# Hymba-style layer on one core: bias rows replicated inside DRAM, set-up moved behind the first projection, down operands in low slots

## The chip, the cores and the metric

One Trainium2 chip, one of its cores. The time is device microseconds (us) of the whole kernel on that core. A matrix product runs on TensorE (PE), elementwise work on VectorE (DVE), ScalarE (ACT) and GpSimd (POOL). In this kernel every transfer is issued by SyncE (SP), on one hardware queue that spreads over the core's 16 DMA engines; the issue order on SP is the order in which each DMA engine gets its packets.

## What is computed

The reference is one decoder layer on 2048 tokens of 1024 features: an input projection, sliding-window attention beside RWKV-7 time mixing, an output projection, and a gated feed-forward part with a causal convolution of width 3. Cut to what matters here:

```python
h = rms_norm(x, norm_mix_pre)
proj = h @ w_in                                   # 1024 x 2560
q, k, v, p = split(proj, (512, 640, 768))         # attention part, then the RWKV part p
attn = sliding_window_sink_attention(q, k, v, rel_bias, sinks)
p = p + (shift(p) - p) * rwkv_shift_mix           # token shift, 14 groups of 128 columns
rw = rwkv7_time_mix(p, w0, w_decay_up, a0, w_iclr_up, w_gate_up, k_k, k_a, r_k, ln_x_g, ln_x_b)
x = x + rms_norm(concat(attn, rw) @ w_out, norm_mix_post)
f = conv_gated_ffn(rms_norm(x, norm_ffn_pre), w_ffn_up, conv_w, conv_b, w_ffn_down)
x = x + rms_norm(f, norm_ffn_post)

# inside the attention: a bias that depends on head and distance alone
bias = rel_bias[t5_bucket(rel)]                   # -1e30 outside the window of 128
```

## The kernel before

The kernel runs in stages. `phase_a` (L403 on) goes over four segments of 512 tokens; each takes 20 projections of 128 columns of `w_in` (eight of them as two halves of 64 columns in the attention part) and builds the inputs of the recurrence. `phase_b` (L900 on) does attention, the recurrence in chunks and the output projection; `phase_d` (L100 on) does the feed-forward product up (L244) and down (L392). The tile scheduler of the language orders the instructions of each engine after the code is written, so the row of an engine is not always the order of the source.

Every float32 product is made of three products of rounded parts: `split` casts a tile to its high part on ACT (L40) and subtracts on DVE to get the low part (L41). One projection `proj` (L544) loads a raw weight tile `wr` of 512 KB (L548, two buffers), splits it into `wh` and `wl`, and runs 24 matmuls into `pj` (L30). The hidden vectors of the segment are split into `hh` and `hl`.

The parts that are touched:

- `bias_lines` (L54 to L65), called at L802 before the first segment, makes one line of 384 bias values for each of 8 heads in `ln` (8 partitions), and L65 writes it 128 times over to DRAM, as `d_line` (8 x 128 x 384, 1.5 MB), with a copy whose source is broadcast from the 8 rows. `phase_b` reads `d_line` at L968, with a pitch of 383, so that each of 128 partitions gets its shifted line.
- The parameter vectors (`rows` L485, transposed at L488 into `vec`, with `half` and `omix` behind) and the low-rank weights `wraw` / `wup` / `wlo` / `wgh` / `wgl` (L500 to L515) are set up in `phase_a` ahead of the first projection.
- `shifted` (L556) evicts a projection on ACT: `ps<-pj` (L560), `t<-pj,omix` (L562). `load_x` (L455) squares, normalizes and transposes a tile of tokens: on ACT the squares `junk<-xt` (L467), on PE the transposes `hx` (L473). The step string loads the next segment's tokens (L464) late in a segment, in the steps x; in segment 0 the scheduler hoists the first of these loads, and the squares behind them, to the kernel's start.
- `pairs` (L648) writes `aa` and `bk` (one buffer each) and stores them with `d_ar` (L667) and `d_bk` (L672). `attn` (L765) makes one projection of the attention part; with i = 0 it transposes on PE (`sm`, L577) and stores `d_va` (L772).
- `dprep` (L159) splits the operands of the down product into slots of a list of big buffers, `OPL` (L134) alternating between two sets; `APL` (L346) names the slots that hold finished sums.

The order of segment 0's steps is this string (L807; z lowrank, K key, D decay, P pairs, V value, a attn, x load of the next tokens):

```python
A_ORDER = "z K D K D P a K D P K D P P x i V x i i i V x i i i V x i i i V i i a a a a a"
```

Of the kernel before, what the change touches and what calls it, by code (L numbers as in the profile page):

```python
# [14 lines left out]
P = 128  # L15
# [6 lines left out]
H = 8  # L22
# [16 lines left out]
def split(nc, hi, lo, raw):  # L39
    nc.scalar.copy(out=hi, in_=raw)  # L40
    nc.vector.tensor_tensor(out=lo, in0=raw, in1=hi, op=ALU.subtract)  # L41
# [9 lines left out]
    return r  # L51


def bias_lines(nc, pool, psum, rel_bias, onehot, neg, line_d):  # L54

    rb = pool("rb")[:32, :H]
    nc.sync.dma_start(out=rb, in_=rel_bias)
    oh = pool("oh")[:32, :384]
    nc.sync.dma_start(out=oh, in_=onehot)
    ln = pool("ln")[:H, :384]  # L60
    nc.sync.dma_start(out=ln, in_=bcast_rows(neg, H))
    pl = psum("pl")[:H, :384]
    nc.tensor.matmul(out=pl, lhsT=rb, rhs=oh, start=True, stop=True)
    nc.vector.tensor_tensor(out=ln, in0=pl, in1=ln, op=ALU.add)
    nc.sync.dma_start(out=line_d, in_=ln[:, None, :].to_broadcast([H, P, 384]))  # L65


def hsum(nc, pool, tag, h2t, hq, k):
# [26 lines left out]
def phase_d(ctx, tc, x1, h2t, w_up, cw, halo, w_down, g_post, mhalf, out, hq, act, td):  # L95
# [8 lines left out]
    with ExitStack() as es:  # L104
# [26 lines left out]
        x1v = x1.rearrange("(t p) d -> t p d", p=P)  # L131
        phases = [(p, k) for p in ORD for k in range(KC)]
        raw, dops = {}, {}
        OPL = ((0, 1, 2), (10, 11, 12))  # L134

        HPL = ((0, 1), (2, 3), (4, 5), (10, 11), (6, 7), (8, 9), (12, 13))

# [201 lines left out]
        with ExitStack() as ds_:  # L339
# [3 lines left out]
            nc.sync.dma_start(out=gpost, in_=bcast_rows(g_post))  # L343
            ssq = fp.tile([P, 2, SEQ // P], F32, name="ssq")
            xts, acc = {}, {}
            APL = {"C22": (3, 4), "C12": (5, 6), "C11": (7, 8)}  # L346

            def xload(t):
                xts[t] = fp.tile([P, D], F32, name="xt", bufs=3)
# [70 lines left out]
def phase_a(ctx, tc, x, g_pre, w_in, vecs, w_decay, w_iclr, w_gate, tri, ident, mhalf, gc, o, bias):  # L420
# [5 lines left out]
    with ExitStack() as es:  # L426
# [50 lines left out]
        for _ in load_x(0):  # L477
            pass


        rows = cp.tile([42, P], F32, name="rows")
        r0 = 0
        for v in vecs:
            n = v.shape[0] // P
            nc.sync.dma_start(out=rows[r0:r0 + n, :], in_=v.rearrange("(j p) -> j p", p=P))  # L485
            r0 += n
        pt = ps_s.tile([P, 512], F32, name="sm")
        nc.tensor.transpose(out=pt[:, :42], in_=rows, identity=ident[:42, :42])  # L488
        vec = cp.tile([P, 42], F32, name="vec")
        nc.vector.tensor_copy(out=vec, in_=pt[:, :42])  # L490
        hw0, ha0, k_k, k_a, r_k, ln_g, ln_b = (vec[:, 4 * i:4 * i + 4] for i in range(7))
        mix = vec[:, 28:42]
        half = cp.tile([P, 12], F32, name="half")
        nc.vector.tensor_scalar(out=half[:, 0:8], in0=vec[:, 0:8], scalar1=0.5, scalar2=None, op0=ALU.mult)
        nc.vector.tensor_scalar(out=half[:, 8:12], in0=k_a, scalar1=0.5, scalar2=None, op0=ALU.mult)
        hw0, ha0, hka = half[:, 0:4], half[:, 4:8], half[:, 8:12]
        omix = cp.tile([P, 14], F32, name="omix")
        nc.vector.tensor_scalar(out=omix, in0=mix, scalar1=-1.0, scalar2=1.0, op0=ALU.mult, op1=ALU.add)

        wl2, wup = [], []  # L500
        for h, w in ((0, w_decay), (1, w_iclr)):
            raw = ep.tile([P, 512], F32, tag="e", name="wraw", bufs=NE)
            nc.sync.dma_start(out=raw[0:64], in_=w)
            nc.sync.dma_start(out=raw[64:128], in_=w)
            hi = cp.tile([P, 512], F32R, name=f"wup{h}")
            nc.scalar.copy(out=hi, in_=raw)
            lo = cp.tile([P, 512], F32R, name=f"wlo{h}")
            nc.vector.tensor_tensor(out=lo, in0=raw, in1=hi, op=ALU.subtract)
            wl2.append(lo)
            wup.append(hi)  # L510
        raw = ep.tile([P, 512], F32, tag="e", name="wraw", bufs=NE)
        nc.sync.dma_start(out=raw, in_=w_gate)
        wgh = cp.tile([P, 512], F32R, name="wgh")
        wgl = cp.tile([P, 512], F32R, name="wgl")
        split(nc, wgh, wgl, raw)  # L515
        ind = cp.tile([P, 2], F32, name="ind")
        bones = cp.tile([P, P], F32, name="bones")
        nc.vector.memset(ind, 0.0)
# [16 lines left out]
        def segment(sb, nxt):  # L535
# [19 lines left out]

            def shifted(i, tag="sh", bufs=5):  # L556
                u = proj([768 + i * P])
                s = ep.tile([P, SB + 1], F32, name="ps", tag="ps", bufs=2)
                nc.scalar.copy(out=s[:, 0:1], in_=halo[:, i:i + 1])
                nc.scalar.copy(out=s[:, 1:], in_=u)  # L560
                t1 = E("t1", tag, bufs)
                nc.scalar.activation(out=t1, in_=u, func=AF.Copy, scale=omix[:, i:i + 1])  # L562
                nc.scalar.copy(out=halo[:, i:i + 1], in_=s[:, SB:])
                nc.vector.scalar_tensor_tensor(out=t1, in0=s[:, :SB], scalar=mix[:, i:i + 1], in1=t1, op0=ALU.mult, op1=ALU.add)
                return t1
# [19 lines left out]

            def lowrank():
                z = shifted(12)
                nc.scalar.activation(out=z[0:64], in_=z[0:64], func=AF.Tanh)
                zw = ep.tile([P, SB], F32R, name="zw")
                za = ep.tile([P, SB], F32R, name="za")  # L590
                nc.scalar.copy(out=zw[0:64], in_=z[0:64])
                nc.vector.tensor_tensor(out=zw[64:128], in0=z[0:64], in1=zw[0:64], op=ALU.subtract)
                nc.scalar.copy(out=za[64:128], in_=z[64:128])
                nc.vector.tensor_tensor(out=za[0:64], in0=z[64:128], in1=za[64:128], op=ALU.subtract)
                z = shifted(13)
                nc.scalar.activation(out=z, in_=z, func=AF.Tanh, scale=0.5)
                nc.vector.tensor_scalar(out=z, in0=z, scalar1=0.5, scalar2=0.5, op0=ALU.mult, op1=ALU.add)
                zgh = ep.tile([P, SB], F32R, name="zgh")
                zgl = ep.tile([P, SB], F32R, name="zgl")
                split(nc, zgh, zgl, z)  # L600
                lr.extend((zw, za, zgh, zgl))

            def decay(hp):
                zw, za = lr[:2]
                fs = slice(hp * P, (hp + 1) * P)
# [12 lines left out]
                ig = E("ig", "e", 6)  # L618
                nc.scalar.activation(out=ig, in_=cum, func=AF.Exp, scale=CDEC)
                nc.gpsimd.tensor_copy(out=gc[:, hp, cs], in_=ga[:, :, C])  # L620

                u = lora((wup[1][:, fs], za), (wl2[1][:, fs], za))
                ta = E("ta", "e", 6)
                nc.scalar.activation(out=ta, in_=u, func=AF.Tanh, scale=0.5, bias=ha0[:, c1])
                held[hp] = ga, ig, ta

            def key(hp):

                c1 = slice(hp, hp + 1)
# [55 lines left out]

            def value(hp):
                zgh, zgl = lr[2:]
                fs = slice(hp * P, (hp + 1) * P)
                c1 = slice(hp, hp + 1)

# [72 lines left out]
                    yield  # L763

            def attn(i):  # L765
                ts = slice(t0, t0 + SB)
                u = proj([[640], [512]][i] if i < 2 else [(i - 2) * 64, 256 + (i - 2) * 64])
                t = E("qkv", "qo", 2)
# [370 lines left out]
def hybrid_layer(ctx, tc, a, c, out):  # L1139
# [6 lines left out]
    nc.vector.memset(mhalf, -0.5)  # L1146
    gc = cp.tile([P, 4, SEQ // C], F32, name="gc")
    s = {k: dp.tile(list(v), F32, name="d_" + k) for k, v in A_OUT.items()}
    line = dp.tile([H, P, 384], F32, name="d_line")
    x1 = dp.tile([SEQ, D], F32, name="d_x1")  # L1150
    h2t = [dp.tile([8, P, SEQ // 2], F32, name=f"d_h2t{j}") for j in range(2)]
# [4 lines left out]
    x = a["x"][0]  # L1156
    vecs = [a[n].rearrange("l h n -> (l h n)") if n == "r_k" else a[n][0] for n in _VECS]
    phase_a(ctx, tc, x, a["norm_mix_pre"], a["w_in"][0], vecs, a["w_decay_up"][0], a["w_iclr_up"][0], a["w_gate_up"][0],
            c["tri"], ident, mhalf, gc, s, (a["rel_bias"], c["onehot"], c["neg"], line))
# [47 lines left out]
```

## Time and profile before

| | |
|---|---|
| median of 3 runs | 3152.18 us (3151.63 to 3157.87) |
| the profiled execution, own time | 3157.18 us |
| its span | 3155.4 us |
| mean granted clock of TensorE | 0.978 |
| PE busy | 3037.6 us, 96% of the span |
| DVE / ACT / POOL busy | 2247.4 (71%) / 1452.0 (46%) / 1093.9 us (35%) |
| DMA traffic | 459.57 MB, 146 GB/s on average |

Times in the rows are of the profiled execution, in us from the start of its span; a group of instructions shows its total busy time and the mean of one in ns. PE leaves only 118 us of the span idle, so a change shows in how much of that it removes or adds, and in where. A bracket such as `[23.05 <-ACT t L562]` in a row of the timeline is idle time of the engine right before the row, and what ended it.

### The profile page before, as it was taken

The numbers are of one execution on the slowest core, as the hardware profiler recorded it, in microseconds if no ns is written. First come the engines' busy times: TensorE is split into PE (matmuls) and PEld (weight loads), VectorE is DVE, ScalarE is ACT, GpSimd is POOL, SyncE is SP. The second block draws the span as 40 slices with busy tenths as digits, with TensorE's granted clock in tenths as the row PEclk, the third lists the DMA queues.
The fourth block names the chain that finished last, engine by engine and source line by source line (L and its number), as shares of the span: only waits on it lengthen the run. The fifth ranks groups of instructions, "written<-read, shape, count | busy, mean of one in ns | idle before, by whom it ended". The sixth has DMA issues, their size and how long they took to land.

```text
span 3155.4 us, 46776 instructions
## 1 busy us (share of the span) xinstructions
PE 3037.6 (96%) x17897; PEld 2450.7 (78%) x17897; DVE 2247.4 (71%) x3171; ACT 1452.0 (46%) x2437; POOL 1093.9 (35%) x903
## 2 busy tenths in 40 slices
PE   5999999989999997999999999999999999999997
PEld 3888888767777775878888877888888888888786
DVE  4778786867666766898888889888888843334555
ACT  4566656444444445444444455444444432333332
POOL 1303020212332533654445444444444420003553
PEclk8999999979999998999999999999999999999999
DMA  5546453663444635443333344333333474436764
GB/s 138 143 131 181 128 164 121 175 188 116 127 126 128 207 112 189 162 134 100 101 101 104 100 139 139 114 100 100 101 100 101 162 276 152 141 140 228 279 213 167
DMA packets 522476, 459.57 MB, mean 146 GB/s; under 512 B 117050, under 2 KB 404108, under 8 KB 521228
## 3 DMA queue, kind: packets, MB, share of 16 engines
q1 hardware_dynamic: 522252, 456.59, 46.1%
q8 instruction: 140, 2.29, 0.3%
q14 instruction: 84, 0.69, 0.1%
HBM read 314.43 MB, written 142.08 MB: 145 GB/s over the span
## 4 chain that ended last, share of the span: by engine, by line
PE 38%; DVE 12%; DMA 4%; issue 4%; ACT 2%; POOL 0%; ACTq 0%; DVEq 0%; POOLq 0%; SPq 0%
PE b L392 19%; PE b L244 19%; DMA wr<-in_w_ffn_up 4%; DVE wl L41 2%; DVE yv L261 2%; DVE yg L262 2%; DVE yv L262 2%; ACT yv L260 1%; DVE yg L287 1%; DVE yg L261 1%; DVE uv L250 1%; DVE hl L41 0%; ACT wh L40 0%; DMA out<-r 0%; DVE halo L258 0%
## 5 line engine op out<-in xcount | busy, mean ns | idle before, releaser
L244 PE MATMUL b<-hh,wh 128*128 128x512 f32 x1792 | 701.2, 393 | 18.3 <-DVE uv L270 10.5
L244 PE MATMUL b<-hl,wh 128*128 128x512 f32 x1792 | 703.1, 392 | 3.0 <-DVE hl L41 3.0
L244 PE MATMUL b<-hh,wl 128*128 128x512 f32 x1792 | 697.9, 392 | 1.6 <-DVE wl L41 1.6
L392 PE MATMUL b<-do 128*128 128x512 f32 x2688 | 615.5, 391 | 5.0 <-DVE do L41 4.2
L392 PEld LDWEIGHTS b<-do 128*128 128x128 f32 x2688 | 506.2, 188 | 113.8 <-DVE do L41 4.7
L41 DVE TENSOR_TENSOR wl<-wr,wh 128x512 fp32r<-128x512 f32 (+1 forms) x400 | 398.8, 1004 | 164.0 <-ACT wh L40 145.8
L40 ACT CAST wh<-wr 128x512 fp32r<-128x512 f32 (+1 forms) x400 | 274.9, 702 | 352.4 <-DMA wr<-in_w_ffn_up 148.1
L244 PEld LDWEIGHTS b<-hh,wh 128*128 128x128 f32 x1792 | 337.5, 188 | 103.8 <-DVE uv L270 21.4
L244 PEld LDWEIGHTS b<-hl,wh 128*128 128x128 f32 x1792 | 337.4, 188 | 77.1 <-DVE hl L41 3.3
L244 PEld LDWEIGHTS b<-hh,wl 128*128 128x128 f32 x1792 | 337.0, 188 | 75.5 <-DVE wl L41 2.8
L41 DVE TENSOR_TENSOR do<-ar,do 128x2048 fp32r<-128x2048 f32 x56 | 130.9, 2337 | 304.6 <-ACT do L40 304.6
L30 PE MATMUL pj<-hh,wh 128*128 128x512 f32 x640 | 257.5, 403 | 27.8 <-ACT t L562 25.1
L40 ACT CAST do<-ar 128x2048 fp32r<-128x2048 f32 x56 | 106.7, 1905 | 358.4 <-PE b L392 338.6
L154 POOL TENSOR_TENSOR br<-br 128x1024 f32<-128x1024 f32 x32 | 100.5, 3141 | 456.2 <-DMA br<-d_td 341.4
L30 PE MATMUL pj<-hh,wl 128*128 128x512 f32 x640 | 255.3, 399 | 0.1
L30 PE MATMUL pj<-hl,wh 128*128 128x512 f32 x640 | 254.3, 398 | 0.0
L221 POOL TENSOR_TENSOR wr<-wr,s 128x512 f32<-128x512 f32 x64 | 139.6, 2181 | 171.4 <-DVE wl L41 164.8
L212 POOL TENSOR_TENSOR s<-wr 128x512 f32<-128x512 f32 x64 | 89.3, 1396 | 277.2 <-DMA wr<-in_w_ffn_up 255.7
L280 ACT ACTIVATE yg<-yg 128x1024 f32<-128x1024 f32 x64 | 67.9, 1061 | 216.7 <-DVE yg L262 216.7
L30 PEld LDWEIGHTS pj<-hh,wh 128*128 128x128 f32 x640 | 122.7, 192 | 56.1 <-ACT t L562 26.8
L261 DVE SCALAR_TENSOR_TENSOR yv<-uv,cw,yv 128x1024 f32<-128x1024 f32 x64 | 125.2, 1957 | 48.9 <-ACT yv L260 48.8
L30 PEld LDWEIGHTS pj<-hh,wl 128*128 128x128 f32 x640 | 122.3, 191 | 27.2 <-DVE wl L41 0.9
(280 smaller groups left out, 5380.8 us busy)
## 6 DMA issues: line engine op xcount, KB each, us to landing
wr<-in_w_ffn_up SPq DMA_DIRECT2D x128, 512.0 KB
ar<-d_act SPq DMA_DIRECT2D x112, 512.0 KB
br<-in_w_ffn_down SPq DMA_DIRECT2D x72, 512.0 KB
wr<-in_w_in SPq DMA_DIRECT2D x64, 512.0 KB
d_act<-sa SPq DMA_DIRECT2D x32, 1024.0 KB
d_act<-yg SPq DMA_DIRECT2D x32, 512.0 KB
xt<-in_x SPq DMA_DIRECT2D x28, 512.0 KB
d_bk<-bk SPq DMA_DIRECT2D x16, 512.0 KB
```

Source lines behind the costliest of these rows:

```text
L30: nc.tensor.matmul(out=out, lhsT=a, rhs=b, start=first and i == 0 and j == 0, stop=last and i == n - 1 and j == 2)
L40: nc.scalar.copy(out=hi, in_=raw)
L41: nc.vector.tensor_tensor(out=lo, in0=raw, in1=hi, op=ALU.subtract)
L154: nc.gpsimd.tensor_tensor(out=br[:, 0], in0=br[:, 0], in1=br[:, 1], op=ALU.subtract)
L212: tt(out=r[1], in0=t[:, 2], in1=t[:, 3], op=ALU.add)
L221: tt(out=t[:, 1], in0=t[:, 1], in1=r[2], op=ALU.subtract)
L244: nc.tensor.matmul(out=o, lhsT=a[:, k, :], rhs=b[:, k, :], start=j in (0, 1, 3) and k == 0 and i == 0, stop=k == 3 and i == 2, skip_group_ ...
L250: nc.vector.tensor_copy(out=u[:, 0:2], in_=halo[:, col, :])
L261: nc.vector.scalar_tensor_tensor(out=y, in0=u[:, 1:SB + 1], scalar=w1c[:, col:col + 1], in1=y, op0=ALU.mult, op1=ALU.add)
L262: nc.vector.scalar_tensor_tensor(out=y, in0=u[:, 0:SB], scalar=w0c[:, col:col + 1], in1=y, op0=ALU.mult, op1=ALU.add)
L280: nc.scalar.activation(out=ys[n], in_=ys[n], func=AF.Gelu_apprx_tanh)
L392: nc.tensor.matmul(out=bks[n], lhsT=x[:, 2 * h + m, a], rhs=b[:, y], start=k == 0 and p not in CHAIN and m == 0 and j == 0, stop=last and ...
```

## The change

Four edits:

1. `bias_lines` becomes a generator. It stores the 8 lines once to DRAM (`d_row`, L65, 12 KB), and then writes `d_line` in four pieces of two heads each, DRAM to DRAM (L68, 384 KB each, the source a row of `d_row` broadcast 128 times). It is advanced by `next(lines, None)` at the head of each `attn`, so in the written order the first `attn` of segment 0 does the set-up and the store, and the next four one piece each.
2. The parameter vectors become `vectors()`, called in the first `shifted` behind its projection; the low-rank weights become `lowrank_weights()`, called in the first `lowrank` behind that.
3. `OPL`'s second set is (4, 5, 6) in place of (10, 11, 12).
4. `APL` moves to (3, 7), (8, 9), (10, 11), so that the sums keep out of the slots of 3.

```diff
-def bias_lines(nc, pool, psum, rel_bias, onehot, neg, line_d):
+def bias_lines(nc, pool, psum, rel_bias, onehot, neg, row_d, line_d):
     ...
     nc.vector.tensor_tensor(out=ln, in0=pl, in1=ln, op=ALU.add)
-    nc.sync.dma_start(out=line_d, in_=ln[:, None, :].to_broadcast([H, P, 384]))
+    nc.sync.dma_start(out=row_d, in_=ln)
+    for h in range(0, H, 2):
+        yield
+        nc.sync.dma_start(out=line_d[h:h + 2], in_=row_d[h:h + 2, None, :].to_broadcast([2, P, 384]))
...
-        OPL = ((0, 1, 2), (10, 11, 12))
+        OPL = ((0, 1, 2), (4, 5, 6))
...
-            APL = {"C22": (3, 4), "C12": (5, 6), "C11": (7, 8)}
+            APL = {"C22": (3, 7), "C12": (8, 9), "C11": (10, 11)}
...
+        ready = {}
+        def vectors():          # the lines that made rows, vec, half, omix, unchanged
+            ...
+            return hw0, ha0, k_k, k_a, r_k, ln_g, ln_b, mix, hka, omix
+        def lowrank_weights():  # the lines that made wup, wlo, wgh, wgl, unchanged
+            ...
+            return wl2, wup, wgh, wgl
...
             def shifted(i, tag="sh", bufs=5):
                 u = proj([768 + i * P])
+                if not ready:
+                    ready["v"] = vectors()
+                mix, omix = ready["v"][7], ready["v"][9]
...
             def lowrank():
                 z = shifted(12)
+                if "w" not in ready:
+                    ready["w"] = lowrank_weights()
...
             def attn(i):
+                next(lines, None)
...
-        bias_lines(nc, E, lambda name: ps_l.tile([P, SB], F32, tag="lo", name=name), *bias)
+        lines = bias_lines(nc, E, lambda name: ps_l.tile([P, SB], F32, tag="lo", name=name), *bias)
...
+    row = dp.tile([H, 384], F32, name="d_row")
     line = dp.tile([H, P, 384], F32, name="d_line")
```

The functions `decay`, `key`, `pairs` and `value` take their vectors and weights from `ready`. Line numbers of the changed kernel are up to 23 higher than those above.

On SP, ahead of the change, the copy stands near the kernel's start, between loads of the weight tiles `wr` and of the next tokens `xt`:

```order
L61 DMA ln<-in_neg 8x384
L548 DMA wr<-in_w_in 128x8x128 x2
L464 DMA xt<-in_x 128x1024 x2
L65 DMA d_line<-ln 1024x1x384
L548 DMA wr<-in_w_in 128x8x128 x2
L464 DMA xt<-in_x 128x1024
L548 DMA wr<-in_w_in 128x8x128
```

Behind the change, the store and the four pieces stand on SP right behind `d_va`, the store of the one `attn` in the middle of segment 0; the eleventh weight tile `wr_1295` is loaded between the third piece and the fourth:

```order
L559 DMA wr_1177<-in_w_in 128x8x128
L795 DMA d_va_73<-vat_642 128x4x128
L65 DMA d_row_77<-ln_603 8x384
L68 DMA d_line_78<-d_row_77 256x1x384 x3
L559 DMA wr_1295<-in_w_in 128x8x128
L68 DMA d_line_78<-d_row_77 256x1x384
L687 DMA d_ar_68<-aa_735 128x8x64
L692 DMA d_bk_69<-bk_736 128x1024
L559 DMA wr_1341<-in_w_in 128x8x128
```

So the scheduler has taken the pieces out of the last projections and to the middle of the segment. On DVE, at the same place of the program, ahead of the change (`bk` is the tile that `d_bk` stores, `wl` a weight tile's low part; here the tenth):

```order
L680 TENSOR_TENSOR mt_760<-pm_743,mask_281 128x512
L671 TENSOR_TENSOR bk_852<-kp_846,ig_715 64x8x64 x2
L661 SCALAR_TENSOR_TENSOR kp_889<-kp_889,t1_800 128x512
L662 TENSOR_SCALAR ta_838<-ta_838 128x512
L41 TENSOR_TENSOR wl_1179<-wr_1176,wh_1178 128x1024
```

and behind the change:

```order
L700 TENSOR_TENSOR mt_761<-pm_744,mask_244 128x512
L691 TENSOR_TENSOR bk_853<-kp_847,ig_716 64x8x64 x2
L681 SCALAR_TENSOR_TENSOR kp_890<-kp_890,t1_801 128x512
L682 TENSOR_SCALAR ta_839<-ta_839 128x512
L41 TENSOR_TENSOR wl_1298<-wr_1295,wh_1297 128x1024
```

The row itself keeps its order; what moved is the weight tile behind it: the subtract of the eleventh tile stands there now, whose load is issued between the third piece and the fourth, and ahead of it the writes of the next `bk`, which must wait until `d_bk` has read the old one.

## Rows read from the trace of the kernel before

**Rows 1.** PE's waits, whole span: what was waited for, total us, times, longest.

```profile
PE pj L30 <- ACT t L562: 25.1, 4, 23.0
...
PE ht L1092 <- DVE h L1085: 10.7, 2, 8.8
...
PE b L392 <- DVE do L41: 4.2, 1, 4.2
...
PE b L392 <- ACT uv L284: 0.7, 1, 0.7
```

**Rows 2.** Timeline of SP's issues: start, duration, issuing engine, line, transfer.

```profile
10.24 0.32 SPq L485 DMA_DIRECT2D rows<-in_rwkv_shift_mix  x1
...
19.36 0.81 SPq L65 DMA_DIRECT2D d_line<-ln  x1
...
21.97 25.99 SPq L548 DMA_DIRECT2D wr<-in_w_in  x2
...
48.06 6.94 SPq L464 DMA_DIRECT2D xt<-in_x  x1
...
104.51 0.36 SPq L772 DMA_DIRECT2D d_va<-vat  x1
```

**Rows 3.** Timeline 37 to 75 us, ACT and PE: start, duration, [idle before].

```profile
59.52 1.06 ACT L467 ACTIVATE junk<-xt 128x1024 f32<-128x1024 f32 x1 [27.76 <-DMA xt<-in_x]
...
61.99 0.69 ACT L562 ACTIVATE t<-pj,omix 128x512 f32<-128x512 f32 x1
...
62.73 0.80 PE L30 MATMUL pj<-hh,wh 128*128 128x512 f32 x1 [23.05 <-ACT t L562]
...
66.36 0.39 PE L30 MATMUL pj<-hl,wh 128*128 128x512 f32 x1
66.59 0.39 PE L30 MATMUL pj<-hh,wl 128*128 128x512 f32 x1
```

**Rows 4.** Stretches: us, busy us of PE, PEld, DVE, ACT, POOL, clock, DMA share, GB/s.

```profile
core 0: us, PE busy (x) PEld busy (x) DVE busy (x) ACT busy (x) POOL busy (x), PEclk, DMA share, GB/s
5.00:8.00 3.00, 0.14 (x1) 0.14 (x2) 1.29 (x1) 0.66 (x3) 0.75 (x2) 1.00 0.98 386
40.00:47.00 7.00, 0.00 (x0) 0.00 (x0) 0.00 (x0) 0.00 (x0) 0.00 (x0) 0.67 0.45 48
62.00:66.00 4.00, 3.13 (x7) 2.03 (x8) 2.70 (x3) 2.00 (x5) 0.00 (x0) 0.50 0.14 40
```

**Rows 5.** Timeline of the middle of segment 0 on PE, 103 to 130 us.

```profile
103.21 0.66 PE L577 MATMUL sm<-ident,qkv 128*128 128x128 f32 x4
...
129.82 0.27 PE L473 MATMUL hx<-ident,xt 128*128 128x128 f32 x1
```

**Rows 6.** DVE's lines, 80 to 140 us: count, busy us, mean ns, idle before.

```profile
L41 DVE TENSOR_TENSOR wl<-wr,wh 128x1024 fp32r<-128x1024 f32 x7 | 8.8, 1256 | 4.2 <-ACT wh L40 4.2
L671 DVE TENSOR_TENSOR bk<-kp,ig 64x512 f32<-64x512 f32 x8 | 6.0, 748 | 0.1
L661 DVE SCALAR_TENSOR_TENSOR kp<-kp,t 128x512 f32<-128x512 f32 x4 | 3.1, 776 | 0.1
L662 DVE TENSOR_SCALAR ta<-ta 128x512 f32<-128x512 f32 x4 | 2.6, 645 | 0.0
```

**Rows 7.** DMA issues of the whole span: transfer, engine, count, size of one.

```profile
wr<-in_w_in SPq DMA_DIRECT2D x64, 512.0 KB
d_bk<-bk SPq DMA_DIRECT2D x16, 512.0 KB
d_ar<-aa SPq DMA_DIRECT2D x16, 256.0 KB
d_line<-ln SPq DMA_DIRECT2D x1, 1536.0 KB
```

**Rows 8.** Timeline of the start, 12 to 29 us, PE and ACT.

```profile
12.13 0.30 PE L488 MATMUL sm<-ident,rows 42*128 42x42 f32 x1 [2.30 <-DMA rows<-in_rwkv_shift_mix]
...
24.34 4.25 ACT L40 CAST hh<-hr 128x512 fp32r<-128x512 f32 x8
...
25.00 1.22 PE L30 MATMUL pj<-hh,wh 128*128 128x512 f32 x2 [2.67 <-ACT hh L40]
```

**Rows 9.** Chain of waits, 2975 to 2990 us, in order of time.

```profile
2978.84 0.74 DVE acc L372
2979.59 1.73 DVE do L41
```

More of the change, by code (lines that the diff above doesn't have):

```diff
@@ L478, in phase_a @@
             pass
[L481 to L498, printed above, removed]
@@ L500, in phase_a @@
-        wl2, wup = [], []
-        for h, w in ((0, w_decay), (1, w_iclr)):
-            raw = ep.tile([P, 512], F32, tag="e", name="wraw", bufs=NE)
[L503 to L515, printed above, removed]
+        ready = {}
+        def vectors():
+            rows = cp.tile([42, P], F32, name="rows")
+            r0 = 0
+            for v in vecs:
+                n = v.shape[0] // P
+                nc.sync.dma_start(out=rows[r0:r0 + n, :], in_=v.rearrange("(j p) -> j p", p=P))
+                r0 += n
+            pt = ps_s.tile([P, 512], F32, name="sm")
+            nc.tensor.transpose(out=pt[:, :42], in_=rows, identity=ident[:42, :42])
+            vec = cp.tile([P, 42], F32, name="vec")
+            nc.vector.tensor_copy(out=vec, in_=pt[:, :42])
+            hw0, ha0, k_k, k_a, r_k, ln_g, ln_b = (vec[:, 4 * i:4 * i + 4] for i in range(7))
+            mix = vec[:, 28:42]
+            half = cp.tile([P, 12], F32, name="half")
+            nc.vector.tensor_scalar(out=half[:, 0:8], in0=vec[:, 0:8], scalar1=0.5, scalar2=None, op0=ALU.mult)
+            nc.vector.tensor_scalar(out=half[:, 8:12], in0=k_a, scalar1=0.5, scalar2=None, op0=ALU.mult)
+            hw0, ha0, hka = half[:, 0:4], half[:, 4:8], half[:, 8:12]
+            omix = cp.tile([P, 14], F32, name="omix")
+            nc.vector.tensor_scalar(out=omix, in0=mix, scalar1=-1.0, scalar2=1.0, op0=ALU.mult, op1=ALU.add)
+            return hw0, ha0, k_k, k_a, r_k, ln_g, ln_b, mix, hka, omix
@@ new lines, in lowrank_weights @@
+        def lowrank_weights():
+            wl2, wup = [], []
+            for h, w in ((0, w_decay), (1, w_iclr)):
+                raw = ep.tile([P, 512], F32, tag="e", name="wraw", bufs=NE)
+                nc.sync.dma_start(out=raw[0:64], in_=w)
+                nc.sync.dma_start(out=raw[64:128], in_=w)
+                hi = cp.tile([P, 512], F32R, name=f"wup{h}")
+                nc.scalar.copy(out=hi, in_=raw)
+                lo = cp.tile([P, 512], F32R, name=f"wlo{h}")
+                nc.vector.tensor_tensor(out=lo, in0=raw, in1=hi, op=ALU.subtract)
+                wl2.append(lo)
+                wup.append(hi)
+            raw = ep.tile([P, 512], F32, tag="e", name="wraw", bufs=NE)
+            nc.sync.dma_start(out=raw, in_=w_gate)
+            wgh = cp.tile([P, 512], F32R, name="wgh")
+            wgl = cp.tile([P, 512], F32R, name="wgl")
+            split(nc, wgh, wgl, raw)
+            return wl2, wup, wgh, wgl
@@ L604, in decay @@
                 zw, za = lr[:2]
+                hw0, ha0 = ready["v"][:2]
+                wl2, wup = ready["w"][:2]
                 fs = slice(hp * P, (hp + 1) * P)
@@ L630, in key @@
                 k = shifted(4 + hp)
+                k_k = ready["v"][2]
                 kk = E("kk", "e", 6)
@@ L652, in pairs @@
                 k, kk, rt = held.pop((hp, "k"))
+                hka = ready["v"][8]
                 u = ps_l.tile([P, NT, P], F32, tag="lo", name="rb")
@@ L687, in value @@
                 zgh, zgl = lr[2:]
+                r_k, ln_g, ln_b = ready["v"][4:7]
+                wgh, wgl = ready["w"][2:]
                 fs = slice(hp * P, (hp + 1) * P)
@@ L1158, in hybrid_layer @@
     phase_a(ctx, tc, x, a["norm_mix_pre"], a["w_in"][0], vecs, a["w_decay_up"][0], a["w_iclr_up"][0], a["w_gate_up"][0],
-            c["tri"], ident, mhalf, gc, s, (a["rel_bias"], c["onehot"], c["neg"], line))
+            c["tri"], ident, mhalf, gc, s, (a["rel_bias"], c["onehot"], c["neg"], row, line))
     kp = ctx.enter_context(tc.tile_pool(name="conv", bufs=1))
```

## The prediction

> **What bounds the kernel now.** I read the page first: PE is busy for 96% of the span, so only two things can move the time, PE's idle stretches and its clock. The sums of PE's waits come next [rows 1]: the largest single one, 23.0 us, is a projection that waits for an eviction on ACT (t, L562). The waits at the down product, which the last two edits touch, are 4.2 and 0.7 us. The timeline around the 23 us tells the rest [rows 3]. ACT had been standing at the square of a token tile of the next segment, 27.76 us, for the load of that tile; the evictions of two projections stood behind it in ACT's row, came at 61.99, and let PE go on at 62.73. [...] From 40 to 47 us the engines were busy to 45% and moved 48 GB/s, where from 5 to 8 us they moved 386 GB/s at 98% [rows 4]. 45% is 7.2 of 16 engines, and the copy's source has 8 rows: each row of the source was one engine's work, the other eight engines idled, and every later load, which has a share on all 16, ended only when the eight were through. So the start of the kernel is bounded by a transfer that uses half the engines, slowly.
>
> **Edit 1, what it removes.** Without the old copy the token tile lands with its neighbours and the 23.05 us go. What is late next is the projection's own work, since the tiles behind it have landed by then. PE also came back at half clock: from 62 to 66 us 0.50 was granted [rows 4], and the seven products from 62.73 to 66.36 took 3.63 us, where they follow each other every 0.23 us right after [rows 3], 1.6 together. So 2.0 us more go, together 25.05 us.
>
> **Edit 1, what it adds.** The order of the changed kernel decides here: the store of the lines and the four pieces stand right behind `d_va`, in the middle of segment 0, not in the last projections. Each piece reads 2 rows of `d_row`, each broadcast 128 times. By what the old copy did with 8 rows, a piece gives its 384 KB to 2 engines, 196.6 KB each, and four pieces queue on the same two. Every load and store behind them has packets on those two engines and waits, however idle the other 14 are.
>
> How long one piece takes (S) is in no row, since the kernel before has no copy inside DRAM. The bounds are the two rates of an engine. Fast: 386 GB/s at 0.98 of 16 engines is 24.6 GB/s for each, 196.6 KB in 8.0 us [rows 4]. Slow: 48 GB/s over the old copy's 8 engines is 6.0 GB/s, 32.8 us [rows 4]. I take 16.0, an estimate: the fast rate, with each byte counted twice, since here DRAM is read and written. It lies nearer to the fast row, because the slow one read 8 neighbouring rows of the chip's own memory, which these pieces don't. A longer S than 8.0 is what I choose; a shorter one no row excludes, but none shows an engine above 24.6 GB/s. The Trainium skill has a price for copies between two DRAM tensors, in "DMA: Bandwidth & Descriptors", section "Latency and other measured facts": 214 GB/s in full over all 16 engines, which would be an estimate of 14.7 us for a piece, and 3175 us by the sum below; no run here shows it, and the sum goes by 16.0.
>
> The sum, from the transposes of the `d_va` tile (103.21 before [rows 5]) as zero:
> - `d_va` is issued 1.30 later and takes 0.36 to issue [rows 2], so `d_row` is issued at 1.7. A small load takes 1.9 from issue to its user (the vector load issued at 10.24 [rows 2], PE at 12.13 [rows 8]): landed at 3.6.
> - The first bytes of the pieces move at 5.1 (of another 1.9, I give 1.5 to the start and 0.4 to the end, an estimate). Four pieces: 5.1 + 4 x 16.0 = 69.1.
> - Behind the pieces stand `wr_1295`, `d_ar` and `d_bk`, 512 + 256 + 512 KB [rows 7], 1.31 MB at 16 x 24.6 = 394 GB/s: 3.3, to 72.4; with the end's 0.4, 72.8.
> - DVE's row has the new writes of `bk` ahead of the low part of the eleventh weight tile. `bk` has one buffer, and its writes wait for `d_bk`, which the pieces hold. Then DVE does two writes of `bk` (0.75 each), one of `kp` (0.78), one of `ta` (0.65) and the subtract (1.26) [rows 6], 4.2 in all: PE gets the eleventh tile's products going at 77.0. On ACT the cast of `wr_1295` stands ahead of the eviction of an earlier projection, so the same loads hold both engines that feed PE; ACT is through before DVE.
> - PE has other work until then: before, from 103.21 to the transposes at 129.82 [rows 5], 26.6 us. The changed order has three products of 0.23 fewer there: 25.9.
> So PE stands 77.0 - 25.9 = 51.1 us, and comes back at half clock as it did at 62.73, 2.0 more: 53.1. Net of the 25.05, **+28.0 us**. It is zero at S = 9.0.
>
> **Edit 2 costs about nothing.** The vectors and low-rank weights are the same instructions behind the first projection. PE's wait for `rows` was 2.30 us [rows 8], but the first projection started at 25.00, 0.66 us after the casts of the hidden vectors began at 24.34 [rows 8], which follow the token loads; the set-up was hidden beside them. With the weight load ahead of it, the set-up is hidden by the 24 matmuls of that projection; if that cover failed, the wait of 2.30 would come back. I take 0, with 3 us either way.
>
> **Edits 3 and 4.** The slots change which earlier product must have left a slot before a split may write it. The product's waits at the start of the down stage can lose 0.7 us at most [rows 1]. The wait of 4.2 is not theirs: the chain shows that split on DVE at 2979.59, straight behind a sum (L372) that ended then [rows 9], inside the stage. I take 0, with 0.7 either way. The scheduler's new order of the rest may move small waits, such as the 10.7 us of the recurrence [rows 1]; I allow 6 us either way, with no sign.
>
> **The time.** The profiled execution took 3157.2 us, 5.0 above the median of the runs. 3157.2 + 28.0 = 3185.2 against the profile, 3180.2 against the median: I say 3180.
>
> **The rivals.** A, the forecast: two engines, S between 12 and 22, 3164 to 3204.
> - B: two engines at the line rate, S = 8.0. PE resumes at 45.0 and stands 19.1 + 2.0 us: net -4.0, 3148. For it speaks that a line of 1536 bytes is no short packet; against it, that both sides are DRAM, which no row shows at that rate.
> - C, slower by far: S = 32.8, as the old copy. The stall is 118.3 + 2.0: net +95.2, 3247. For it: the only copy of this very shape in the trace ran at that rate. Against it: its source was eight partitions side by side, here it is DRAM.
> - D, the faster side: the pieces spread over 16 engines, or land beside the loads without holding them. Then four pieces take 1.57 MB at 394 GB/s, 4.0 us, inside PE's 25.9 of other work, and the 25.05 are a plain gain: 3127. It decides from S of about 3. For it: fewer bytes are read from the chip's memory, and a write into DRAM has no reason in the rows to keep to two engines. Against it: 45% for 8 rows [rows 4]. The Trainium skill's rule in "DMA: Bandwidth & Descriptors", section "Rules for kernel authors", is that an outermost dimension of c keeps a transfer on at most c engines; by it D falls, and the trace agrees for c = 8.
> - That the change doesn't do what it says: it does not, as the pieces stand in mid-segment. Were they run late, in the last projections, with free engines, D's time would come out; the order rules this out, so it has no chance of its own.
>
> **How the numbers follow.** A 0.50, B 0.22, C 0.10, D 0.18. A difference of 0.2%, 6.3 us, is about what a measurement of this kernel can tell from none; within it is 3145.9 to 3158.5. B lies there for most of its range; I give 0.18 of it to "same" and 0.04 to "faster". Faster: 0.18 + 0.04 = 0.22; same 0.18; slower 0.60. The range goes from D with 3 us of ripple, 3124, to the top of A with 2 us, 3206. It leaves out C and the edges of A and D, less than 0.2. A alone is 3164 to 3204.
>
> **What would show it.** In the profile after, between about 105 and 160 us: a stretch of some 60 us with a DMA share near 2/16 = 0.125; ACT standing for tens of us at the cast of a weight tile, for its load; DVE standing at the write of `bk`, for `d_bk`; PE idle about 51 us there, and then at half clock for some 3.6 us. Near 40 us, no square that waits 27 us, and no wait of 23 us at PE. If PE's idle time there is near 20 us, it is B; near 118, C; if there is none, D, and my step from 8 source rows to 8 engines is wrong. If the start still shows the 23 us, the old copy was not what held the token tile, and the whole gain falls.

## The result and the profile after

The changed kernel takes 3188.2 us (median of 4 runs, 3183.15 to 3192.22) against 3152.55 us before (4 runs, 3151.63 to 3157.87): a ratio of 1.0109, 95% interval 1.009 to 1.0127. It is slower by 35.6 us. The time lies inside the forecast range, 8 us above the forecast of 3180. But the traces show that the number came out by luck: each piece took half the time that the forecast gave it, so the pieces cost 18 us (run 3 below) in place of 53, and a stage of which it said nothing costs the rest.

PE's waits, whole span, of the kernel after (what was waited for, total us, times, longest), answer to [rows 1]:

```profile
PE b L247 <- DVE uv L273: 36.4, 24, 2.9
...
PE pj L30 <- DVE wl L41: 8.8, 1, 8.8
PE b L247 <- ACT wh L40: 8.4, 2, 7.7
PE pj L30 <- ACT t L576: 7.0, 5, 5.4
```

The 23 us of [rows 1] are gone. In their place stand 8.8 and 5.4 us in the middle of segment 0, and a new first row: 36.4 us in the feed-forward up product, in 24 waits for an add on DVE. Before, that row was the third:

```profile
PE b L244 <- DVE uv L270: 10.5, 14, 1.9
```

Where the time went shows in the first start of the up product (L244, after L247) and of the down product (L392, after L395). The views of these lines, before (x count: ns least/median/most, first and last start in us):

```profile
L244 PE MATMUL b<-hh,wh x1792: 387/389/763, 1257.6 to 2527.2; 128*128 128x512 f32 x200
```

```profile
L392 PE MATMUL b<-do x2688: 387/389/792, 2507.3 to 3138.1; 128*128 128x512 f32 x192
```

and after:

```profile
L247 PE MATMUL b<-hh,wh x1792: 387/389/796, 1255.2 to 2563.6; 128*128 128x512 f32 x200
```

```profile
L395 PE MATMUL b<-do x2688: 387/389/628, 2539.2 to 3168.4; 128*128 128x512 f32 x192
```

All that stands ahead of the up stage, segment 0 with its pieces included, ends 2.4 us earlier than before. That is no more than two executions of the same order differ by: run 2 below, which is the kernel before up to there, enters the up stage at 1254.5. Segment 0 alone ends 2.65 us earlier (the first projection product of segment 1 starts at 188.89 us, before at 191.54). The up stage takes 2539.2 - 1255.2 = 1284.0 us where it took 1249.7. The down stage takes 629.2 for 630.8. So the whole loss, 34 us, is in a stage that none of the four edits is about. The stretches of that stage, before and after (columns as in [rows 4]):

```profile
1257.60:2507.30 1249.70, 1231.32 (x5329) 1000.24 (x5330) 1076.56 (x1207) 604.86 (x899) 599.46 (x330) 1.00 0.36 114
1255.20:2539.20 1284.00, 1244.01 (x5329) 1007.71 (x5330) 1106.91 (x1206) 611.09 (x900) 596.79 (x328) 0.99 0.36 111
```

PE runs the same 5329 products. It is idle for 40.0 us in place of 18.4, which is 21.6 of the loss, and busy for 12.7 us more.

**The start and the middle of segment 0.** The stretches that answer to [rows 4], after (columns as there):

```profile
40.00:47.00 7.00, 7.00 (x32) 5.76 (x32) 3.74 (x6) 6.43 (x16) 0.52 (x2) 1.00 0.76 221
```

```profile
90.00:95.00 5.00, 5.00 (x24) 4.04 (x23) 4.94 (x9) 4.23 (x8) 0.00 (x0) 1.00 0.13 48
95.00:100.00 5.00, 5.00 (x53) 3.98 (x52) 2.56 (x4) 1.73 (x3) 0.59 (x2) 1.00 0.13 50
...
110.00:115.00 5.00, 1.73 (x6) 1.44 (x7) 0.00 (x0) 2.20 (x4) 0.00 (x0) 0.59 0.34 96
115.00:120.00 5.00, 0.77 (x4) 0.36 (x2) 0.00 (x0) 0.00 (x0) 0.00 (x0) 0.50 0.75 232
```

At 40 to 47 us PE is busy throughout, where it stood. While the pieces run, the DMA share is 0.13, which is 2 of 16 engines, and 48 to 50 GB/s: some 24.5 GB/s for each of the two, so a piece of 196.6 KB for each takes 8.0 us. In the trace, the first three pieces land 7.8 us apart (93.8, 101.6, 109.4 us). The timeline of this place, all engines, after:

```profile
79.71 0.66 PE L591 MATMUL sm<-ident,qkv 128*128 128x128 f32 x4
...
83.44 11.03 SPq L68 DMA_DIRECT2D d_line<-d_row  x3
94.58 7.65 SPq L559 DMA_DIRECT2D wr<-in_w_in  x1
102.27 3.90 SPq L68 DMA_DIRECT2D d_line<-d_row  x1
...
111.09 1.04 ACT L40 CAST wh<-wr 128x1024 fp32r<-128x1024 f32 x1 [12.91 <-DMA wr<-in_w_in]
...
113.27 0.79 PE L30 MATMUL pj<-hh,wh 128*128 128x512 f32 x1 [5.37 <-ACT t L576]
...
120.99 1.39 DVE L691 TENSOR_TENSOR bk<-kp,ig 64x512 f32<-64x512 f32 x2 [21.45 <-DMA d_bk<-bk]
...
123.33 1.22 DVE L41 TENSOR_TENSOR wl<-wr,wh 128x1024 fp32r<-128x1024 f32 x1
124.61 0.79 PE L30 MATMUL pj<-hh,wl 128*128 128x512 f32 x1 [8.84 <-DVE wl L41]
```

This is the chain of the forecast, link by link: SP's issues back up behind the pieces, ACT's cast waits 12.9 us for the weight tile, DVE's write of `bk` waits 21.45 us for `d_bk`, PE gets the low part's products at 124.61. That is 44.9 us after the transposes at 79.71; the rival B had 45.0. PE stands 5.4 + 8.8 = 14.2 us, and the clock is 0.50 to 0.59 from 110 to 120 us.

**The up stage.** One unit of the steady part, DVE and POOL, and PE's wait behind it, after:

```profile
1547.41 2.28 POOL L221 TENSOR_TENSOR wr<-wr 128x512 f32<-128x512 f32 x1
1548.45 1.78 DVE L41 TENSOR_TENSOR wl<-wr,wh 128x512 fp32r<-128x512 f32 x1
...
1550.23 1.21 DVE L290 TENSOR_TENSOR yg<-yg,yv 128x1024 f32<-128x1024 f32 x1
1551.37 0.16 DVE L253 COPY uv<-halo 128x2 f32<-128x2 f32 x1
1551.44 1.27 DVE L264 SCALAR_TENSOR_TENSOR yg<-ug,cw,yg 128x1024 f32<-128x1024 f32 x1
1551.53 2.31 POOL L302 TENSOR_TENSOR sa<-yg 128x512 f32<-128x512 f32 x1 [1.84 <-DVE uv L253]
1552.63 1.75 DVE L41 TENSOR_TENSOR wl<-wr,wh 128x512 fp32r<-128x512 f32 x1
1554.31 0.68 DVE L273 TENSOR_TENSOR uv<-sum,b 128x512 f32<-128x512 f32 x1
...
1555.04 0.80 PE L247 MATMUL b<-hh,wh 128*128 128x512 f32 x1 [2.94 <-DVE uv L273]
...
1556.80 0.68 DVE L41 TENSOR_TENSOR wl<-wr,wh 128x512 fp32r<-128x512 f32 x1
```

The same place of the unit before:

```profile
1541.08 1.27 DVE L250 COPY uv<-halo 128x2 f32<-128x2 f32 x1
1542.27 1.27 DVE L262 SCALAR_TENSOR_TENSOR yg<-ug,cw,yg 128x1024 f32<-128x1024 f32 x1
1542.29 2.40 POOL L299 TENSOR_TENSOR sa<-yg 128x512 f32<-128x512 f32 x1
1543.46 0.68 DVE L270 TENSOR_TENSOR uv<-sum,b 128x512 f32<-128x512 f32 x1
1544.06 1.19 DVE L41 TENSOR_TENSOR wl<-wr,wh 128x512 fp32r<-128x512 f32 x1
```

The add `uv<-sum,b` reads a bank of PSUM into which PE's next product of the unit adds, so PE can't go on before it. Before, the weight subtract (L41) stands behind the add; after, ahead of it, and there it takes 1.75 us beside POOL's `sa<-yg`. Before, it began late in that instruction of POOL and took 1.19; with POOL idle it takes 0.68 (at 1556.80). In the new row every second unit of the first token half makes PE stand 1.2 to 2.95 us. After the wait above PE comes back at a granted clock of 0.50, the lower of its two levels:

```profile
1555.00:1558.00 3.00, 2.96 (x7) 2.39 (x8) 3.00 (x5) 1.09 (x2) 0.80 (x1) 0.50 0.00 0
1561.00:1564.00 3.00, 3.00 (x15) 2.49 (x14) 2.23 (x3) 1.84 (x3) 0.46 (x1) 1.00 0.68 172
```

Seven products take the 3 us in which 15 run later; so such a wait costs more than its length, and part of the longer busy time of the stage is of this kind. The scheduler has given the stage this row: the code of the stage is the same. Why it orders the stage otherwise for edits so far ahead is not shown.

### The profile page after: what moved, and what is told of

Same layout as the page of the kernel before. It is cut to its first block, busy times and chain, and to the rows that moved or that the text cites. A ratio compares the mean times of both kernels' runs of the same rounds, so it can differ in the third digit from the quotient of the medians.

```text
span 3185.9 us, 46722 instructions
## 1 busy us (share of the span) xinstructions
PE 3046.7 (96%) x17897; PEld 2457.1 (77%) x17897; DVE 2274.3 (71%) x3170; ACT 1456.5 (46%) x2438; POOL 1085.6 (34%) x903
## 4 chain that ended last, share of the span: by engine, by line
PE 69%; DVE 16%; DMA 6%; issue 4%; ACT 4%; POOL 1%; SPq 1%; DVEq 0%; ACTq 0%; POOLq 0%
PE b L247 19%; PE b L395 17%; PE pj L30 13%; PE m L30 6%; DMA wr<-in_w_ffn_up 3%; DVE wl L41 3%; DVE yv L265 2%; PE pp L892 2%; DVE yg L265 2%; DVE yv L264 2%; DVE yg L264 1%; DVE yg L290 1%; PE po L1059 1%; ACT yv L263 1%; PE lo L584 1%
## 5 line engine op out<-in xcount | busy, mean ns | idle before, releaser
L247 PE MATMUL b<-hh,wh 128*128 128x512 f32 x1792 | 705.4, 396 | 47.7 <-DVE uv L273 36.4
L247 PE MATMUL b<-hl,wh 128*128 128x512 f32 x1792 | 706.5, 394 | 0.0
L247 PE MATMUL b<-hh,wl 128*128 128x512 f32 x1792 | 703.7, 395 | 0.0
L395 PE MATMUL b<-do 128*128 128x512 f32 x2688 | 612.6, 390 | 6.5 <-DVE do L41 5.1
L395 PEld LDWEIGHTS b<-do 128*128 128x128 f32 x2688 | 505.4, 188 | 113.0 <-DVE do L41 6.0
L41 DVE TENSOR_TENSOR wl<-wr,wh 128x512 fp32r<-128x512 f32 (+1 forms) x400 | 426.2, 1070 | 156.3 <-ACT wh L40 150.1
L247 PEld LDWEIGHTS b<-hh,wh 128*128 128x128 f32 x1792 | 339.7, 190 | 138.1 <-DVE uv L273 52.2
L247 PEld LDWEIGHTS b<-hl,wh 128*128 128x128 f32 x1792 | 340.4, 190 | 74.3
L247 PEld LDWEIGHTS b<-hh,wl 128*128 128x128 f32 x1792 | 339.8, 190 | 73.9
L41 DVE TENSOR_TENSOR do<-ar,do 128x2048 fp32r<-128x2048 f32 x56 | 135.5, 2419 | 303.0 <-ACT do L40 303.0
L215 POOL TENSOR_TENSOR s<-wr 128x512 f32<-128x512 f32 x64 | 98.2, 1534 | 400.6 <-DMA wr<-in_w_ffn_up 375.6
L224 POOL TENSOR_TENSOR wr<-wr,s 128x512 f32<-128x512 f32 x64 | 115.3, 1801 | 181.8 <-DVE wl L41 179.0
L264 DVE SCALAR_TENSOR_TENSOR yv<-uv,cw,yv 128x1024 f32<-128x1024 f32 x64 | 115.2, 1801 | 49.6 <-ACT yv L263 49.2
L30 PEld LDWEIGHTS pj<-hh,wl 128*128 128x128 f32 x640 | 122.5, 191 | 35.6 <-DVE wl L41 9.2
```

Source lines behind the costliest of these rows:

```text
L30: nc.tensor.matmul(out=out, lhsT=a, rhs=b, start=first and i == 0 and j == 0, stop=last and i == n - 1 and j == 2)
L215: tt(out=r[1], in0=t[:, 2], in1=t[:, 3], op=ALU.add)
L224: tt(out=t[:, 1], in0=t[:, 1], in1=r[2], op=ALU.subtract)
L247: nc.tensor.matmul(out=o, lhsT=a[:, k, :], rhs=b[:, k, :], start=j in (0, 1, 3) and k == 0 and i == 0, stop=k == 3 and i == 2, skip_group_ ...
L264: nc.vector.scalar_tensor_tensor(out=y, in0=u[:, 1:SB + 1], scalar=w1c[:, col:col + 1], in1=y, op0=ALU.mult, op1=ALU.add)
L395: nc.tensor.matmul(out=bks[n], lhsT=x[:, 2 * h + m, a], rhs=b[:, y], start=k == 0 and p not in CHAIN and m == 0 and j == 0, stop=last and ...
```

## The experiments

Two questions: is it the row that costs the 34 us, and were the pieces slow because of two engines? Where a kernel's row is held, a table of positions, taken from the order of the named kernel, adds edges between neighbours on PE, DVE, ACT and POOL, for the up stage alone. Such an edge sets the order and waits for nothing. SP is not held, but its order in the stage follows: in run 1 it is that of the kernel before, in run 2 that of the changed kernel. Each ratio is against the kernel before as run beside it (medians of 3153.58, 3155.21 and 3154.31 us).

**1. The changed kernel with the old row of the up stage.**

```diff
+def in_row(tc, first):
+    info = mybir.DependencyInfo(mybir.DependencyClass.NoSync, mybir.DependencyReason.DATA)
+    ...
+        for p, q in zip(row, row[1:]):
+            tc.add_manual_dep(q, p.name, info, reason="row")
```

> The changed kernel, with the instructions of the feed-forward up stage held on PE, DVE, ACT and POOL in the row that they have in the kernel before (edges without waits; nothing else differs). In the two traces the up stage of the changed kernel is 35 us longer, and its start comes 2.4 us earlier. Theory 1, the row: the scheduler's new row of the up stage, which none of the four edits is about, costs the 35 us; then this kernel gives back all of it, 3152 to 3156 us, and PE's wait for the add into uv falls from 36.4 to about 10 us. Theory 2, the entry: the stage runs longer because it is entered at another moment against DMA and clock, and the row is innocent; then the time stays at 3185 to 3190.

3156.18 us against 3153.58 before, ratio 1.0007 (0.9997 to 1.0018): all but some 3 us come back. PE's waits and the two lines' views:

```profile
PE b L247 <- DVE uv L273: 12.8, 17, 1.8
```

```profile
L247 PE MATMUL b<-hh,wh x1792: 387/389/765, 1258.0 to 2535.4; 128*128 128x512 f32 x200
```

```profile
L395 PE MATMUL b<-do x2688: 387/389/792, 2510.9 to 3140.4; 128*128 128x512 f32 x192
```

The up stage takes 1252.9 us. It is entered at 1258.0, as late as before, with all four edits in place: the row decides, not the entry.

**2. The kernel before with the new row.** The same function, with the changed kernel's order in the table.

```diff
+    first = len(nc.cur_bb.bb.instructions)
     phase_d(ctx, tc, x1, h2t, ...
+    in_row(tc, first)
```

> The kernel before, with the up stage held on the same four engines in the row of the changed kernel. None of the four edits is in it. Theory 1, the row: 3152.5 + 35 = 3185 to 3190 us, with the wait for the d_line copy (23 us of PE near 40 us) still there and PE's wait for the add into uv near 36 us. Theory 2, the entry: 3152 us, as before.

3183.72 us, ratio 1.0087 (1.0071 to 1.0104). None of the four edits is in it, and it loses 30.1 us:

```profile
PE b L244 <- DVE uv L270: 37.2, 24, 2.8
PE pj L30 <- ACT t L562: 23.6, 4, 21.5
```

The add's waits are those of the changed kernel, and the copy's wait at the start is still there. Theory 1, that the row costs the time, holds from both sides.

**3. The pieces over 16 engines.**

```diff
-        nc.sync.dma_start(out=line_d[h:h + 2], in_=row_d[h:h + 2, None, :].to_broadcast([2, P, 384]))
+        nc.sync.dma_start(out=line_d[h:h + 2].rearrange("h p n -> p h n"), in_=row_d[None, h:h + 2, :].to_broadcast([P, 2, 384]))
```

> The changed kernel, with the 128 copies as the outermost dimension of each piece in place of the two heads; the rows of all engines stay as they are. If a piece was slow because it went to two engines: the four pieces take 4 us in place of 31, PE's 14 us of idle time near 105 to 125 us and its half clock there go, and the time is 3188 - 15 to 18 = 3170 to 3173 us. If a copy inside DRAM from a repeated row is slow whatever the engines: the pieces still hold the loads, and the time stays at 3185 to 3190.

3169.88 us, ratio 1.0045 (1.0029 to 1.0061): 18.3 us less than the changed kernel. In the stretch of the pieces:

```profile
84.00:90.00 6.00, 6.00 (x35) 4.90 (x34) 3.92 (x8) 2.42 (x6) 1.95 (x2) 1.00 0.75 210
```

The share is 0.75 where it was 0.13, and from 80 to 120 us PE is busy all the time. SP issues the weight load in 0.55 us, where it took 7.65 behind the slow pieces:

```profile
85.56 0.55 SPq L559 DMA_DIRECT2D wr<-in_w_in  x1
```

So the same bytes at the same place cost PE nothing when all engines carry them.

**4. Both at once**, the old row and 16 engines: the diffs of runs 1 and 3 together.

> Both at once: the changed kernel, the up stage in its old row, and the pieces over 16 engines. If the two costs are separate and each theory above holds: 3153 - 16 = 3134 to 3140 us, faster than both kernels. If the row is innocent: 3170. If the pieces' shape is innocent: 3153.

3138.06 us, ratio 0.995 (0.9932 to 0.9969), faster than both kernels: the two costs are separate and add up (-32.0, -18.3; together -50.1).

**5. One swap on DVE, in the new row.** Every second unit of the first half:

```diff
-wl<-wr,wh    (L41)
 uv<-sum,b    (L273)
+wl<-wr,wh    (L41)
```

> The changed kernel with its own row of the up stage, but for one swap of neighbours on DVE in 16 units of the first token half: the add into uv, which PE's next product into the same bank waits for, stands ahead of the subtract of a weight tile (L41) that stood right before it. In the trace of the changed kernel that subtract takes 1.75 us there, beside work on POOL, and PE stands 1.2 to 2.95 us in every second unit, 14 times. Theory, the late add: each of these waits shrinks by 1.75 us or to nothing, 23 us together, 3188 - 23 = 3165 us. Rival, DVE is simply too full in the new row: the weight tile is then the late one, PE waits for it instead, and the time stays at 3183 to 3190.

3177.85 us, ratio 1.0076 (1.0061 to 1.0091): 10 us come back, not 23.

```profile
PE b L247 <- DVE uv L273: 30.8, 31, 3.7
```

The waits in the swapped units shrink from some 2.2 to 0.85 us, but the units between them, which had none, now wait some 1.0 us, where the add stands behind a pass of `yg` of 2.3 us. The theory named the right place and was too simple: the time taken away in one unit brought the next one's add too late.

**6. Edits 3 and 4 alone.** The kernel before with

```diff
-        OPL = ((0, 1, 2), (10, 11, 12))
+        OPL = ((0, 1, 2), (4, 5, 6))
...
-            APL = {"C22": (3, 4), "C12": (5, 6), "C11": (7, 8)}
+            APL = {"C22": (3, 7), "C12": (8, 9), "C11": (10, 11)}
```

> The kernel before with edits 3 and 4 alone, the slots of the down operands. By the prediction they are worth nothing, 0.7 us at most either way: 3152 to 3154 us. They leave the row of the up stage as it was. Rival: the lower slots are free later or earlier than the high ones, and the 4.2 us wait in the down stage changes: up to 4 us either way.

3153.51 us, ratio 0.9997 (0.9988 to 1.0007). Worth nothing, as forecast; the up stage keeps its row.

**7. Edit 2 alone.** The kernel before with `vectors()` and `lowrank_weights()`, defined as in the change:

```diff
                 u = proj([768 + i * P])
+                if not ready:
+                    ready["v"] = vectors()
...
                 z = shifted(12)
+                if "w" not in ready:
+                    ready["w"] = lowrank_weights()
```

> The kernel before with edit 2 alone, the set-up behind the first projection; the d_line copy stays as it was. The scheduler gives the up stage the new row here too, though the edit ends some 1200 us earlier. Theory, the row: 3152.5 + 29 to 33 = 3182 to 3186 us, all of it lost between 1400 and 1850 us, while the start is within 3 us of before. Rival: the set-up costs time itself, and the start is late by 5 us or more.

3185.29 us, ratio 1.0097 (1.0081 to 1.0114). Segment 0 ends 1.5 us earlier than before and the up stage takes 1284.3 us: the edit costs nothing where it stands, and some 30 us where the scheduler carries it. The copy's wait at the start only changes its name:

```profile
PE pj L30 <- ACT wh L40: 24.9, 1, 24.9
```

**8. In the old row, with 16 engines, the add moved ahead** of the pass of `yg` that stood before it, in 56 units.

```diff
-yg<-ug,cw,yg (L265)
 uv<-sum,b    (L273)
+yg<-ug,cw,yg (L265)
```

> The kernel of the old row with 16 engines for the pieces, and on DVE in 56 units the add into uv moved ahead of the convolution pass of yg that stands right before it, which takes 1.27 us, and 2.3 to 2.4 beside work on POOL. With the old row PE still waits some 11 to 13 us for that add, 17 times. Theory, the late add: most of it goes, 3138 - 8 = 3130 us. Rival, the pass is late in its turn and the sum is nothing: 3136 to 3140.

3131.73 us, ratio 0.9929 (0.9914 to 0.9944), 6.3 us below run 4. PE's wait for the add is nearly gone:

```profile
PE b L247 <- DVE uv L273: 0.7, 2, 0.5
```

**9. In the new row, the add further ahead**: of a pass of `yg` in 56 units, and in 16 of them of the subtract too; one of the 16:

```diff
-yg<-ug,cw,yg (L264)
-wl<-wr,wh    (L41)
 uv<-sum,b    (L273)
+yg<-ug,cw,yg (L264)
+wl<-wr,wh    (L41)
```

> The changed kernel with its own row of the up stage, and on DVE the add into uv further ahead: in the 16 units of the earlier swap ahead of the subtract and of the first pass of yg, in 40 others ahead of the second pass of yg, which takes 2.3 us there beside POOL. After the earlier swap PE waited about 0.85 us in the swapped units and about 1.0 us in the units between them, 31 times and 30.8 us in all, where the add stood behind such a pass. Theory, the late add in both kinds of unit: nearly all of the 31 us go, 3178 - 25 = 3150 to 3157 us. Rival, DVE too full in this row: the passes and subtracts behind it are late instead, and the time stays above 3170.

3173.58 us, ratio 1.006 (1.0043 to 1.0076). The forecast of 3150 to 3157 missed; the rival had it.

```profile
PE b L247 <- DVE uv L273: 18.0, 16, 1.7
PE b L247 <- ACT sum L277: 9.7, 20, 0.6
```

18 of the 36 us of add waits remain, and ACT's copies of the sums are late in their turn, which before made PE wait nowhere. Moving this one add recovers some 16 of the up stage's 34 us (1267 us from first up to first down product, where it was 1284 and before 1250). Which other differences between the rows make the other half is open.

**10. The old place of the copy, 16 engines.**

```diff
-    nc.sync.dma_start(out=line_d, in_=ln[:, None, :].to_broadcast([H, P, 384]))
+    nc.sync.dma_start(out=row_d, in_=ln)
+    nc.sync.dma_start(out=line_d.rearrange("h p n -> p h n"), in_=row_d[None].to_broadcast([P, H, 384]))
```

> The kernel before with one edit at the old place of the copy: the lines are stored once to DRAM, and d_line is written from there in one transfer with the 128 copies outermost. The up stage keeps its old row. If the copy's eight engines were what held the token tile and PE's 23 us: the waits near 40 us go, 3153.5 - 15 to 25 = 3129 to 3138 us. If the copy was not the cause: 3150 to 3156.

3129.86 us, ratio 0.992 (0.9906 to 0.9935): 24.4 us faster than before. The PE wait of 23 us is gone, nothing was moved, and the up stage keeps its row.

**11. Edit 1 alone.** The kernel before with the generator and its calls, as in the change:

```diff
+    for h in range(0, H, 2):
+        yield
+        nc.sync.dma_start(out=line_d[h:h + 2], in_=row_d[h:h + 2, None, :].to_broadcast([2, P, 384]))
...
             def attn(i):
+                next(lines, None)
```

> The kernel before with edit 1 alone, the four pieces of two heads behind the store of d_va; the scheduler gives the up stage nearly the new row (60 lines of DVE's differ from it). The gain at the start, 25 us, and the loss to the pieces, 20 to 22, leave -3 to -5; the row costs 30 to 32: 3153.5 + 27 = 3179 to 3183 us. If edit 2 had a part in the loss, this kernel would be faster than that by as much.

3196.53 us, ratio 1.0132 (1.0117 to 1.0147): some 15 us more than expected. The timeline shows part of it: with edit 2 left out, all four pieces stand ahead of the weight tile, and PE's products of the `pairs` step wait for `bk` too.

```profile
120.69 1.04 ACT L40 CAST wh<-wr 128x1024 fp32r<-128x1024 f32 x1 [18.98 <-DMA wr<-in_w_in]
122.80 1.39 DVE L674 TENSOR_TENSOR bk<-kp,ig 64x512 f32<-64x512 f32 x2 [19.21 <-DMA d_bk<-bk]
...
127.17 0.45 PE L681 MATMUL pm<-aa,bk 64*64 64x64 f32 x2 [15.73 <-DVE bk L673]
```

Segment 0 ends at 192.7 us where the changed kernel ended it at 188.9, the rest up to the up stage is 6.7 us longer, and the up stage takes 1282.7 us. In that rest PE's idle time is no longer (41 us for 43); its busy time is, by 8 us, and why is open. The loss in the up stage is there without edit 2, and by run 7 with edit 2 alone: either edit brings a new order. So their costs don't add (30 us in run 7, 42 here, 36 for all four).

**12. Run 10 with the add ahead**, in 56 units of the old row: the diffs of runs 10 and 8.

> The kernel with the copy on 16 engines at its old place, and on DVE the add into uv ahead of the pass of yg before it, in 56 units of the old row. From the two parts: 3153.5 - 22 - 6 = 3122 to 3130 us, faster than both kernels. If the parts overlap, no better than either alone: 3130.

3123.32 us, ratio 0.99 (0.9885 to 0.9915), the fastest of all: 65 us less than the changed kernel.

## Why the prediction came out, and where it was wrong

- **The gain at the start**, 25.05 us: right. The 81st projection product starts at 72.03 us before and at 47.24 after, 24.8 less; run 10, which has this gain alone, is 24.4 us faster.
- **The pieces' place and their two engines**: right, from the order and from the row of 45% [rows 4]. DMA share 0.13, and run 3 takes the cost away by the shape alone.
- **The time of one piece**, 16.0 us: wrong. This is the term of the sum that was mis-sized, and it measured 7.8 to 8.0, the fast bound of 8.0 from [rows 4]. The step "each byte counted twice, since here DRAM is read and written" is what failed: an engine that copies inside DRAM moved 24.5 GB/s here, as one that loads. The Trainium skill ("DMA: Bandwidth & Descriptors", "Latency and other measured facts") has 214 GB/s as the full rate of copies between DRAM tensors, of tiles of 128 rows of 16 KiB. Taken as the work of 16 engines that is an estimate of 13.4 for each, and the 14.7 us of the prediction were worked out from it. With two engines the trace shows nearly twice that rate, and the measurement decides. With 8.0, the forecast's own sum gave rival B: PE on again at 45.0 (measured 44.9), net -4.0. Measured: segment 0 ends 2.65 us earlier than before. B's stall of 19.1 us is 14.2 us in the trace, for two reasons: PE's other work lasted 28.2 us (to 107.9) in place of 25.9, and 2.5 us of products ran between the two waits. The 44.9 hide both. The pieces' whole cost is 18.3 us in run 3; in the traces segment 0 ends 17.4 us earlier there (171.49 us), 14.3 less idle time of PE and 3.2 less busy time.
- **Edit 2, nothing; edits 3 and 4, nothing**: right where they stand (run 7 up to the up stage, run 6).
- **"The scheduler's new order of the rest may move small waits; I allow 6 us either way"**: wrong, and this decided the result. The up stage lost 34.3 us in the trace; taking the old row gives back 32.0 us (run 1), and the new row alone costs 30.1 (run 2). The forecast looked at the order around the pieces and not at the later stages, though the order of the up stage was there to be compared, and the third row of PE's waits before already named the add on DVE as the tightest thing in it (10.5 us).
- So +28.0 for edit 1 stood for about nothing there (2.65 us less by the end of segment 0, 2.6 us more in the time of run 1, which has all four edits and the old row) and for +30 to +34 elsewhere. Two errors of about the same size cancelled: the size of the result is luck. The chance of 0.60 for slower rested on a case that didn't happen; of the cases as priced, B came true in segment 0, and its time of 3148 would have been the forecast with the right S. Then the result would have lain 40 us beyond it.

## What to carry to other kernels

Where a scheduler orders the program, compare the order of every stage, not only of the edited one: here a set-up edit that ends more than 1000 us earlier changed the row of another stage and cost some 30 us, and the row can be held by edges that don't wait. In that comparison look for the instruction that frees what the busiest engine needs next, and for what now stands ahead of it. And give a transfer an outermost dimension that all engines can share: the same 1.5 MB cost 25 us at the old place, about 18 us as pieces of two rows, and nothing that shows on 16 engines.

## What the runs showed of the hardware

- Two DMA engines that copy inside DRAM, in lines of 1536 bytes, moved 48 to 50 GB/s, 24.5 each, the rate of a load; the old copy's eight, from eight neighbouring rows of the chip's memory, moved 48 together [rows 4].
- A DVE subtract with two inputs in the chip's memory took 0.68 us with POOL idle (1556.80 above) and 1.75 to 1.78 beside POOL (1548.45 and 1552.63). The add that has one of its inputs in PSUM kept its time through the whole stage (the last row below), in which POOL was busy for 597 of 1284 us. The Trainium skill, "SBUF — State Buffer", section "Who interferes with whom", says that a DVE instruction with two SBUF inputs contends with a POOL instruction that reads SBUF, that the one that comes second blocks until the first is done, and that one with a single SBUF input, outside its two-port modes, doesn't contend. The trace agrees: the subtract at 1548.45 ends at 1550.23, some 0.5 us after POOL's instruction that began at 1547.41 and took 2.28, and the 64 adds stay between 670 and 689 ns.
- After PE had waited 2.94 us for the add, the granted clock was 0.50 for the next 3 us, and 7 products ran in place of 15.

The adds of the stage, after (x count: ns least/median/most, first and last start in us):

```profile
L273 DVE TENSOR_TENSOR uv<-sum,b x64: 670/675/689, 1282.0 to 2556.6; 128x512 f32<-128x512 f32 x64
```
